# Low-rank products of a recurrent token mixer: from inside the scan to the input projection, through DRAM

## The chip, the cores and the metric

The kernel runs on one core of a Trainium2 chip. TensorE multiplies matrices into PSUM, VectorE and ScalarE work on tiles in SBUF and PSUM, GpSimd (POOL) does a few elementwise steps, and the queue of SyncE (SP) issues nearly every transfer between DRAM and SBUF. Each engine takes its instructions in a fixed order and waits on semaphores. The metric is the device time of one execution in microseconds (us), as the median of several runs.

## The reference

One layer, 2048 tokens of width 1024, in float32. The input is normed and multiplied with one input matrix; its columns are r, k, v (768 each), the low-rank inputs of decay and rate (64 each) and of the gate (128), and the queries of a small cross-attention (256). The first 2560 columns are mixed with the token before. What the change concerns:

```
log_w = -softplus(-(w0 + tanh(wd) @ w2)) - 0.5
decay = exp(-exp(log_w))
a = sigmoid(a0 + ad @ a2)
g = sigmoid(gd) @ g2
k = k * (1.0 + (a - 1.0) * k_a)
y = delta_rule_scan(r, decay, k, v, -kk, kk * a)
return (group_norm(y) * lnx_g + lnx_b + bonus) * g
```

The scan is a state of 64 x 64 in each of 12 heads, updated token by token. Scan and cross-attention go through an output matrix onto the residual stream, then an MLP of width 4096 follows.

## The kernel before

The tokens are cut three ways: 4 groups of 512 for the dense products, 16 pairs of 128 for the scan's preparation, and 32 chunks of 64 for the state update. `project(g)` multiplies a group with 22 column blocks (pz, L102, three float32r products of split operands, 24 matmuls of 512 columns a block), and `shift_store` mixes in the token before and stores a block to DRAM: r and k to rk_d, v to v_d, block 18 (decay and rate, split in a high and a low part) to lin_d, block 19 (gate) to sg_d, blocks 20 and 21 to q_d. A scheduler places every instruction by a priority number; `dense` gives the projections 1 to 3 and the output products fixed places among the pairs (`CUTS`, in steps of 640 numbers a pair), and `prepare` runs at a raised priority.

`prepare(p)` loads r (R) and k (KT) of a pair. At every second pair it loads lin for 256 tokens, multiplies it with the decay and rate matrices (pl, L324) and takes a tanh (th, L326); cs and tha are the halves of th that belong to the pair. From cs come the cumulated decay (L330 to L337), from both the operands AR and BK (L349 to L374), then the products pp (L390), a 32-step triangular inverse on VectorE (zt and Zw, L431 and L435) by way of DRAM (nd, Ti, zdr, Z), and more small products. `scan` does the two state updates (prhs, pw, pS at L485 to L498; S at L501 and L502). `post` forms the pair's result, transposes it (pty), adds a bias on ScalarE (mixT, L559), multiplies the stored gate input SG with the gate matrix in plain float32 (pg, L563) and multiplies the two on VectorE (L565). `output` multiplies by the output matrix (pout, L629). PSUM pools: psx (3 buffers) for the dense products, psa (2) for `prepare`, psy (1) for `post`. The small SBUF tiles of the projection share 7 buffers (`small`).

Of the kernel before, what the change touches and what calls it, by code (L numbers as in the profile page):

```python
# [60 lines left out]
def hybrid_layer(  # L61
# [75 lines left out]

    rk_d = [dram.tile([2 * NB, P, G], F32, name=f"rk_d{g}") for g in range(NG)]
    v_d = [dram.tile([G, MW], F32, name=f"v_d{g}") for g in range(NG)]
    lin_d = [dram.tile([2, P, G], F32, name=f"lin_d{g}") for g in range(NG)]  # L140
    sg_d = [dram.tile([P, G], F32, name=f"sg_d{g}") for g in range(NG)]
    q_d = [dram.tile([2, P, G], F32, name=f"q_d{g}") for g in range(NG)]
    mem_d = [dram.tile([P, 2, G], F32, name=f"mem_d{g}") for g in range(NG)]
    mix_d = [dram.tile([P, NB, G], F32, name=f"mix_d{g}") for g in range(NG)]
# [52 lines left out]
    bc = lambda a: a.unsqueeze(2).to_broadcast([a.shape[0], a.shape[1], HD])  # L197
    K = {}

    def scan_setup():  # L200
        K["kkc"] = col(rw_k_k[0], "kkc")
        kac = col(rw_k_a[0], "kac")
        K["lbc"] = col(rw_lnx_b[0], "lbc")
        K["ka2"] = ka2 = cb.tile([P, NB], F32, name="ka2")
        nc.vector.tensor_scalar_mul(ka2, kac, 0.5)
        K["ka1"] = ka1 = cb.tile([P, NB], F32, name="ka1")
        nc.vector.tensor_scalar(ka1, kac, -0.5, 1.0, ALU.mult, ALU.add)
        K["lgr"] = lgr = cb.tile([P, MW], F32, name="lgr")
        nc.sync.dma_start(lgr, rw_lnx_g.to_broadcast([P, MW]))

        K["lora"], K["lob"] = [], []
        for which, (w2, w0) in enumerate(((rw_w2, rw_w0), (rw_a2, rw_a0))):
            src = pr.tile([P, MW], F32, tag="kk", name="lsrc")
            for o in range(2):
                nc.sync.dma_start(src[o * HD : (o + 1) * HD], w2[0])
            wt = cb.tile([P, MW], F32R, name=f"lora{which}")
            lo = pr.tile([P, MW], F32R, tag="EM", name="llo")
            nc.scalar.copy(wt[:HD], src[:HD])
            nc.scalar.copy(lo[HD:], src[HD:])
            nc.vector.tensor_tensor(wt[HD:], src[HD:], lo[HD:].bitcast(F32), op=ALU.subtract)  # L220
            K["lora"].append(wt)
            b0 = col(w0[0], f"lob{which}")
            nc.vector.tensor_scalar_mul(b0, b0, 0.5)
            K["lob"].append(b0)

        K["sel2"] = sel2 = cb.tile([96 + NH, MW], BF16, name="sel2")
        nc.gpsimd.memset(sel2, 0.0)
# [6 lines left out]
                                    fill=0.0, base=HD - 1, channel_multiplier=HD)  # L234
        K["rn3"] = rn3 = cb.tile([96 + NH, P], BF16, name="rn3")
        nc.gpsimd.memset(rn3, 0.0)
        K["g2s"] = g2s = cb.tile([P, MW], F32, name="g2s")
        nc.sync.dma_start(g2s, rw_g2[0])
        K["rkm"] = rkm = cb.tile([P, NB, 2], F32, name="rkm")
        nc.vector.memset(rkm, 0.0)  # L240
        rk_src = rw_r_k[0].rearrange("(b two) d -> two d b", two=2)
# [39 lines left out]
    def prepare(p):  # L281
# [4 lines left out]
        nc.sync.dma_start(R, rk_d[g][:NB, :, tsl].rearrange("b p t -> p b t"))  # L286
        KT = ld.tile([P, NB, P], F32, name="KT")
        nc.sync.dma_start(KT, rk_d[g][NB:, :, tsl].rearrange("b p t -> p b t"))
        if p % 2 == 0:

            L = ld.tile([P, 2, 2, 2 * P], F32R, name="lin")
            for o in range(2):
                for part in range(2):
                    nc.sync.dma_start(L[o * HD : (o + 1) * HD, :, part, :].bitcast(F32),
                                      lin_d[g][part, :, t0 : t0 + 2 * P].rearrange("(a p) t -> p a t", p=HD))

        pss = psa.tile([96 + NH, P], F32, tag="a", name="pss")[96:]
        for b in range(NB):
# [14 lines left out]
        nc.scalar.copy(rn3[1], rn2)  # L313


        if p % 2 == 0:
            K["th"] = []
            for which in range(2):
                t = pr.tile([P, 2, NB, P], F32, name=f"th{which}")
                for b in range(NB):  # L320
                    if b % 2 == 0:
                        pz = psa.tile([P, 2, 2 * P], F32, tag="a", name="pl")
                    for part in range(2):
                        nc.tensor.matmul(pz[:, b % 2, :], K["lora"][which][:, b * P : (b + 1) * P],  # L324
                                         L[:, which, part, :], start=(part == 0), stop=(part == 1))
                    nc.scalar.activation(t[:, :, b, :], pz[:, b % 2, :].rearrange("p (j t) -> p j t", j=2),  # L326
                                         AF.Tanh, scale=0.5, bias=K["lob"][which][:, b : b + 1])
                K["th"].append(t)
        cs, tha = (t[:, p % 2] for t in K["th"])
        nc.vector.tensor_scalar_add(cs, cs, 1.0)  # L330
        for b in range(0, NB, 2):
            csh = flat(cs[:, b : b + 2, :])
# [172 lines left out]

    def post(p, d, states):
        g, t0 = p // 4, (p % 4) * P
        SG = ld.tile([P, P], F32, name="SG")
        nc.sync.dma_start(SG, sg_d[g][:, t0 : t0 + P])
        Vn = ld.tile([P, MW], F32, name="Vn")  # L510
        nc.sync.dma_start(Vn, v_d[g][t0 : t0 + P, :])
        yc = mx.tile([P, NH, HD], F32, name="yc")
# [38 lines left out]
        for q in range(2):  # L551
            bsl = slice(3 * q, 3 * q + 3)
            pt = psy.tile([P, 3, P], F32, tag="y", name="pty")
            for i in range(3):
                b = 3 * q + i
                nc.tensor.transpose(pt[:, i, :], yf[:, b * P : (b + 1) * P], ident)
            for i in range(3):
                b = 3 * q + i
                nc.scalar.activation(mixT[:, b, :], pt[:, i, :], AF.Identity, bias=K["lbc"][:, b : b + 1])  # L559
            pg = psy.tile([P, 3, P], F32, tag="y", name="pg")  # L560
            for i in range(3):
                b = 3 * q + i
                nc.tensor.matmul(pg[:, i, :], K["g2s"][:, b * P : (b + 1) * P], SG,  # L563
                                 start=True, stop=True)
            nc.vector.tensor_tensor(mixT[:, bsl, :], mixT[:, bsl, :], pg, op=ALU.mult)  # L565
        nc.sync.dma_start(mix_d[g][:, :, t0 : t0 + P], mixT)


# [65 lines left out]
    def project(g):  # L634
# [11 lines left out]
                tc.cur_priority -= UPX  # L646
            tc.cur_priority += UPX
        tail = None
        for b in range(NPB):
            w, wh, wl = weights()  # L650
            if g == 0 or (g == 1 and b >= NST):
                load_w(w, rw_in[0][:, b * P : (b + 1) * P], w_d[b] if g == 1 or b < NST else None, g == 0)
            else:
                for i in range(WQ):
                    nc.sync.dma_start(w[i].bitcast(F32), w_d[b][:, i])
            pz = psx.tile([P, G], F32, tag="x", name="pz")
            steps = mm3_steps(pz, wh, wl, lambda k: xh[k // 4][:, k % 4], lambda k: xl[k // 4][:, k % 4], KB)
            for k, _ in enumerate(steps):
                if k == 4 and tail is not None:
                    tail()  # L660
                    tail = None
                yield
            tail = shift_store(g, b, pz)
        if tail is not None:
            tail()

    def shift_store(g, b, pz):

# [15 lines left out]
        elif b < 18:  # L684
# [6 lines left out]
                c0 = (b - 12) * P  # L691
                nc.sync.dma_start(v_d[g][:, c0 : c0 + P].rearrange("(t p) c -> p t c", p=P), vt)
            return rows
        elif b == 18:
            nc.scalar.activation(sl[:HD, :], sl[:HD, :], AF.Tanh)
            hi, lo = small([P, G], "lih", F32R), small([P, G], "lil", F32R)
            split(sl, hi, lo)
            nc.sync.dma_start(lin_d[g][0], hi.bitcast(F32))
            nc.sync.dma_start(lin_d[g][1], lo.bitcast(F32))
        else:  # L700
            nc.scalar.activation(sl, sl, AF.Tanh, scale=0.5)
            nc.vector.tensor_scalar(sl, sl, 0.5, 0.5, ALU.mult, ALU.add)
            nc.sync.dma_start(sg_d[g], sl)
        return None


# [434 lines left out]
```

## Time and profile before

| | |
|---|---|
| median of 3 runs | 2777.49 us (2774.64 to 2781.78) |
| the profiled execution's own time | 2781.47 us |
| its span, first to last instruction | 2779.8 us |
| mean granted TensorE clock | 0.956 |
| TensorE busy | 2620.1 us, 94% |
| VectorE busy | 1807.5 us, 65% |
| ScalarE busy | 1410.8 us, 51% |
| DMA engines busy with the main queue | 60.0% |

Busy shares are means over stages that differ. The rows further down are read by stretches of time: an engine's busy time in a stretch, the clock granted to TensorE there (1.00 is 2.4 GHz), and what an engine waited for.

### The profile page before, as it was taken

The page shows a single profiled execution, that of the slowest core. Times are in us where ns is not written, and L with a number is a line of the kernel's source. Part 1 is how long each engine was busy: PE and PEld are TensorE (multiplying, and loading weights), DVE is VectorE, ACT ScalarE, POOL GpSimd, SP SyncE. Part 2 cuts the span into 40 slices and gives each one's busy share as a digit, 9 for nine tenths or more (in the row PEclk, how much of TensorE's full clock was granted, in tenths as well). Part 3 has the DMA queues.
Part 4 walks back from the last instruction along what each step waited for, and adds up shares of the span by engine and source line. Part 5 has one row for each costly group of instructions (what it writes and reads, how often), then busy time and mean ns, then how long its engine had stood idle before and what let it go on. Part 6 is the DMA issues. An engine that isn't in the chain of part 4 may idle for free.

```text
span 2779.8 us, 49460 instructions
## 1 busy us (share of the span) xinstructions
PE 2620.1 (94%) x17620; PEld 2131.9 (77%) x17620; DVE 1807.5 (65%) x4500; ACT 1410.8 (51%) x3053; POOL 413.1 (15%) x236
## 2 busy tenths in 40 slices
PE   6989999999899998997996999999999999999999
PEld 4777777777677777777885888878888888888887
DVE  4556657676866666778568777765875666655564
ACT  5564456465645547363446444444744444544443
POOL 2002133425304241333111000000100000000000
PEclk9999999999989988798997999999999999999999
DMA  8987564665454544335574576786775444456675
GB/s 251 286 263 215 166 176 135 168 174 165 135 152 138 144 126 120 100 86 164 160 241 133 201 260 244 275 306 191 246 258 170 145 144 155 150 192 208 211 252 167
DMA packets 468444, 519.35 MB, mean 187 GB/s; under 512 B 117538, under 2 KB 291682, under 8 KB 468196
## 3 DMA queue, kind: packets, MB, share of 16 engines
q1 hardware_dynamic: 468196, 516.18, 60.0%
q8 instruction: 139, 2.28, 0.3%
q14 instruction: 109, 0.89, 0.1%
HBM read 361.86 MB, written 154.14 MB: 186 GB/s over the span
## 4 chain that ended last, share of the span: by engine, by line
PE 74%; DMA 10%; DVE 9%; ACT 2%; issue 2%; SPq 2%; POOL 1%; DVEq 0%; ACTq 0%; POOLq 0%
PE pu L964 23%; PE py L1073 22%; PE pz L102 12%; PE pout L629 5%; PE pp L390 2%; DVE zt L431 1%; DVE Zw L435 1%; DMA zdr<-Zw 1%; PE prhs L485 1%; DMA qt<-q_d 1%; DMA KT<-rk_d 1%; DMA Z<-zdr 1%; DMA xt<-in_x_dram 1%; DMA ws<-in_rw_in_dram 1%; PE py L522 1%
## 5 line engine op out<-in xcount | busy, mean ns | idle before, releaser
L102 PE MATMUL pz<-xh,w 128*128 128x512 f32 x1408 | 484.9, 413 | 4.5 <-DVE last L681 2.7
L1073 PE MATMUL py<-wpl,hhh 128*128 128x512 f32 x896 | 349.3, 390 | 0.0
L1073 PE MATMUL py<-wph,hhl 128*128 128x512 f32 x896 | 348.3, 389 | 0.0
L1073 PE MATMUL py<-wph,hhh 128*128 128x512 f32 x896 | 344.0, 391 | 0.0
L102 PEld LDWEIGHTS pz<-xh,w 128*128 128x128 f32 x1408 | 268.9, 193 | 71.8 <-issue 6.6
L93 DVE TENSOR_TENSOR hhl<-hr,hhh 128x512 fp32r<-128x512 f32 x224 | 154.7, 691 | 225.6 <-ACT hhh L92 225.5
L92 ACT CAST hhh<-hr 128x512 fp32r<-128x512 f32 x224 | 139.1, 621 | 311.1 <-PE py L1073 295.5
L102 PE MATMUL pz<-xl,w 128*128 128x512 f32 x704 | 287.7, 409 | 0.4 <-DVE xl L93 0.4
L629 PE MATMUL pout<-wo,xh 128*128 128x256 f32 x1024 | 218.7, 307 | 18.9 <-DVE wo L93 9.6
L431 DVE TENSOR_TENSOR zt<-Ti,Zw 96x96 f32<-96x96 f32 (+20 forms) x736 | 171.2, 256 | 69.3 <-DMA Ti<-nd 49.7
L397 POOL TENSOR_TENSOR PT<-PT,msk 64x768 f32<-64x768 f32 x64 | 178.6, 2790 | 131.4 <-ACT PT L392 129.1
L629 PEld LDWEIGHTS pout<-wo,xh 128*128 128x128 f32 x1024 | 174.5, 205 | 28.9 <-DVE wo L93 12.3
L1073 PEld LDWEIGHTS py<-wph,hhl 128*128 128x128 f32 x896 | 168.4, 188 | 35.0
L1073 PEld LDWEIGHTS py<-wph,hhh 128*128 128x128 f32 x896 | 168.4, 188 | 34.8 <-DVE u L999 0.2
L1073 PEld LDWEIGHTS py<-wpl,hhh 128*128 128x128 f32 x896 | 168.4, 188 | 34.6
L435 DVE TENSOR_TENSOR Zw<-Zw,zt 96x96 f32<-96x96 f32 (+20 forms) x736 | 161.2, 242 | 6.7
L102 PEld LDWEIGHTS pz<-xl,w 128*128 128x128 f32 x704 | 135.8, 193 | 29.8 <-issue 1.9
L93 DVE TENSOR_TENSOR wpl<-wr,wph 128x512 fp32r<-128x512 f32 x224 | 153.3, 684 | 3.8 <-ACT wph L92 3.8
L629 PE MATMUL pout<-wo,xl 128*128 128x256 f32 x512 | 153.1, 299 | 0.0
L86 POOL TENSOR_TENSOR nr<-nm,nhalf 128x1 f32<-128x1 f32 x34 | 28.1, 827 | 789.2 <-DVE nm L84 736.3
L92 ACT CAST wph<-wr 128x512 fp32r<-128x512 f32 x224 | 138.2, 617 | 8.5 <-PE pu L964 7.5
L390 PE MATMUL pp<-AR,BK 64*128 64x128 f32 x768 | 94.5, 322 | 18.5 <-ACT PT L392 16.3
(293 smaller groups left out, 5640.5 us busy)
## 6 DMA issues: line engine op xcount, KB each, us to landing
w<-w_d SPq DMA_DIRECT2D x264, 256.0 KB, 4.0
hr<-hc_d SPq DMA_DIRECT2D x224, 256.0 KB, 2.8
ws<-in_w_ff_dram SPq DMA_DIRECT2D x32, 1024.0 KB, 5.7
hc_d<-hs SPq DMA_DIRECT2D x128, 256.0 KB, 2.2
wr<-t_d SPq DMA_DIRECT2D x128, 256.0 KB, 3.1
wr<-in_w_ff_dram SPq DMA_DIRECT2D x96, 256.0 KB, 3.0
w_d<-w SPq DMA_DIRECT2D x88, 256.0 KB, 4.2
ws<-in_w_out_dram SPq DMA_DIRECT2D x80, 256.0 KB, 4.3
```

The lines of the kernel that those rows point to most:

```text
L86: nc.gpsimd.tensor_tensor(t1, t0, nhalf[: ssum.shape[0], :n], op=ALU.pow)
L92: nc.scalar.copy(hi, src)
L93: nc.vector.tensor_tensor(lo, src, hi.bitcast(F32), op=ALU.subtract)
L102: nc.tensor.matmul(ps, a(k), b(k), start=(k == 0 and i == 0), stop=(k == nk - 1 and i == 2))
L390: nc.tensor.matmul(pps[q][:, j, :], BK[c][rs, b, :], d["AR"][rs, b, :], start=True, stop=True)
L397: nc.gpsimd.tensor_tensor(PT[o : o + C, :, w:], PT[o : o + C, :, w:], K["msk"][o : o + C, w:].unsqueeze(1).to_broadcast([C, NH, 2 * C - w] ...
L431: nc.vector.tensor_tensor(zt[:, j0:j1, :nt], Ti[:, s, s + 1 :].unsqueeze(1).to_broadcast([96, j1 - j0, nt]), Zw[:, j0:j1, s : s + 1].to_br ...
L435: nc.vector.tensor_tensor(Zw[:, j0:j1, s + 1 :], Zw[:, j0:j1, s + 1 :], zt[:, j0:j1, :nt], op=ALU.add)
L485: nc.tensor.matmul(pc[rs, h // 2, :], PT[:, head(h), :C], WV[:, h * HD : (h + 1) * HD], start=True, stop=True)
L629: nc.tensor.matmul(po[:, t, :], a(k, t), w[k][:, b], start=(k == 0 and i == 0 and t == 0), stop=(k == KB - 1 and i == 2 and t == 1))
L964: nc.tensor.matmul(ps, a[u][:, k * P : (k + 1) * P], b[v][:, k, :], start=(first and k == 0 and i == 0), stop=(k == 3 and i == 2), skip_gr ...
L1073: nc.tensor.matmul(ps[bk], a[u][:, m * P : (m + 1) * P], b[v], start=(fresh and c == 0 and t == 0), stop=(c == NCH - 1 and t == 2), skip_g ...
```

## The change

The products of decay, rate and gate with their low-rank matrices leave `prepare` and `post`. A new generator `low_rank(g)` does them once for a group's 512 tokens inside `project(g)`: it reads the stored block back (lw, two buffers), multiplies in psx buffers, and stores tanh and gate to DRAM (th_d, g_d). `prepare` then loads cs and tha, and `post` loads GT. The gate product is now three float32r products of split operands; so block 19 is stored in two parts too. In projections 1 to 3 blocks 18 and 19 come first, and one step of two blocks of low-rank products follows in each later block; in projection 0 the order of blocks stays, so most steps come after block 21. The part of the setup that loads the low-rank matrices moves to block 12 of projection 0.

```
-        if p % 2 == 0:
-            L = ld.tile([P, 2, 2, 2 * P], F32R, name="lin")
-            for o in range(2):
-                for part in range(2):
-                    nc.sync.dma_start(L[o * HD : (o + 1) * HD, :, part, :].bitcast(F32),
-                                      lin_d[g][part, :, t0 : t0 + 2 * P].rearrange("(a p) t -> p a t", p=HD))
+        cs = ld.tile([P, NB, P], F32, name="cs")
+        nc.sync.dma_start(cs, th_d[g][0, :, :, tsl].rearrange("b p t -> p b t"))
+        tha = ld.tile([P, NB, P], F32, name="tha")
+        nc.sync.dma_start(tha, th_d[g][1, :, :, tsl].rearrange("b p t -> p b t"))
...
-        if p % 2 == 0:
-            K["th"] = []
-            for which in range(2):
-                t = pr.tile([P, 2, NB, P], F32, name=f"th{which}")
-                for b in range(NB):
-                    if b % 2 == 0:
-                        pz = psa.tile([P, 2, 2 * P], F32, tag="a", name="pl")
-                    for part in range(2):
-                        nc.tensor.matmul(pz[:, b % 2, :], K["lora"][which][:, b * P : (b + 1) * P],
-                                         L[:, which, part, :], start=(part == 0), stop=(part == 1))
-                    nc.scalar.activation(t[:, :, b, :], pz[:, b % 2, :].rearrange("p (j t) -> p j t", j=2),
-                                         AF.Tanh, scale=0.5, bias=K["lob"][which][:, b : b + 1])
-                K["th"].append(t)
-        cs, tha = (t[:, p % 2] for t in K["th"])
...
-        SG = ld.tile([P, P], F32, name="SG")
-        nc.sync.dma_start(SG, sg_d[g][:, t0 : t0 + P])
+        GT = ld.tile([P, NB, P], F32, name="GT")
+        nc.sync.dma_start(GT, g_d[g][:, :, t0 : t0 + P].rearrange("b p t -> p b t"))
...
-            pg = psy.tile([P, 3, P], F32, tag="y", name="pg")
-            for i in range(3):
-                b = 3 * q + i
-                nc.tensor.matmul(pg[:, i, :], K["g2s"][:, b * P : (b + 1) * P], SG,
-                                 start=True, stop=True)
-            nc.vector.tensor_tensor(mixT[:, bsl, :], mixT[:, bsl, :], pg, op=ALU.mult)
+            nc.vector.tensor_tensor(mixT[:, bsl, :], mixT[:, bsl, :], GT[:, bsl, :], op=ALU.mult)
...
-        for b in range(NPB):
+        low = None
+        for b in list(range(NPB)) if g == 0 else [18, 19] + list(range(18)) + [20, 21]:
+            if g == 0 and b == 12:
+                low_rank_setup()
...
+                if k == 6 and low is not None:
+                    next(low, None)
                 yield
             tail = shift_store(g, b, pz)
+            if b == 19:
+                low = low_rank(g)
+        for _ in low:
+            pass
...
+    def low_rank(g):
+        def pair(hi, lo, rows):
+            t = [ep.tile([P, G], F32R, tag="lw", name="lw", bufs=2) for _ in range(2)]
+            for u, src in zip(t, (hi, lo)):
+                for o in range(0, P, rows):
+                    nc.sync.dma_start(u[o : o + rows].bitcast(F32), src)
+            return t
+        for which in range(2):
+            rs = slice(which * HD, which * HD + HD)
+            xin = pair(lin_d[g][0, rs], lin_d[g][1, rs], HD)
+            for b in range(NB):
+                pl = psx.tile([P, G], F32, tag="x", name="pl")
+                for part in range(2):
+                    nc.tensor.matmul(pl, K["lora"][which][:, b * P : (b + 1) * P], xin[part],
+                                     start=(part == 0), stop=(part == 1))
+                t = small([P, G], "th")
+                nc.scalar.activation(t, pl, AF.Tanh, scale=0.5, bias=K["lob"][which][:, b : b + 1])
+                nc.sync.dma_start(th_d[g][which, b], t)
+                if b % 2 == 1:
+                    yield
+        gin = pair(lin_d[g][2], lin_d[g][3], P)
+        for b in range(NB):
+            pg = psx.tile([P, G], F32, tag="x", name="pg")
+            bs = slice(b * P, (b + 1) * P)
+            for i, (u, v) in enumerate(((0, 0), (0, 1), (1, 0))):
+                nc.tensor.matmul(pg, K["g2"][u][:, bs], gin[v], start=(i == 0), stop=(i == 2))
+            t = small([P, G], "gt")
+            nc.scalar.copy(t, pg)
+            nc.sync.dma_start(g_d[g][b], t)
+            if b % 2 == 1:
+                yield
```

The scheduler decides where these instructions come to stand. On SP's queue at the start of the scan, the program before has this order (lin is the low-rank input of pairs 0 and 1, w the weights and xt the rows of x for projection 1):

```order
L703 DMA sg_d_79<-sl 128x512
L294 DMA lin<-lin_d_75 64x2x256 x2
...
L655 DMA w<-w_d_151 128x512 x4
L655 DMA w<-w_d_152 128x512 x2
L640 DMA xt<-in_x_dram 128x1024
L655 DMA w<-w_d_152 128x512 x2
L672 DMA q_d_83<-sl 128x512
L640 DMA xt<-in_x_dram 128x1024
```

The changed program has this order there; lw is the stored low-rank input, th_d the stored tanh, g_d the stored gate, cs, tha and GT their loads for the pairs:

```order
L665 DMA lw<-lin_d_75 64x512 x4
L295 DMA cs<-th_d_79 128x6x128
L678 DMA th_d_79<-th 128x512 x3
L665 DMA lw<-lin_d_75 128x512 x2
L678 DMA th_d_79<-th 128x512 x3
L297 DMA tha<-th_d_79 128x6x128
L689 DMA g_d_83<-gt 128x512 x6
L623 DMA xt<-in_x_dram 128x1024
L295 DMA cs<-th_d_79 128x6x128
L497 DMA GT<-g_d_83 128x6x128
L293 DMA KT<-rk_d_67 128x6x128
L623 DMA xt<-in_x_dram 128x1024
```

The last two loads of x for projection 1 have moved behind group 0's low-rank loads and stores, and the very last one behind the second pair's cs and the first pair's GT.

On TensorE at the same place, from the last low-rank product to the first pair's pp, the program before has:

```order
L324 MATMUL pl<-lin,lora_1952 128x256 x10
L160 MATMUL pt<-ident,xt 128x128 x8
...
L160 MATMUL pt<-ident,xt 128x128 x4
L102 MATMUL pz<-xh,w 128x512
...
L102 MATMUL pz<-xh,w 128x512
L390 MATMUL pp<-AR,BK 128x128 x6
```

and the changed one:

```order
L674 MATMUL pl<-lw,lora_1172 128x512 x12
L510 MATMUL py_7096<-S,AR 64x64
L686 MATMUL pg<-lw,g2h 128x512 x4
...
L161 MATMUL pt<-ident,xt 128x128 x16
L378 MATMUL pp<-AR,BK 128x128 x6
L393 MATMUL psb<-rkm,tha 64x2 x12
...
L161 MATMUL pt<-ident,xt 128x128 x4
L102 MATMUL pz<-xh,w 128x512
```

Before, 31 matmuls of the next projection (pz) stand ahead of the first pp; now none does, and the gate products stand there. Further on, the scan has moved forward against the dense work: of 384 pS matmuls 264 stood ahead of the last pz and now 288 do, and of the output's matmuls (pout) 692 stood behind the last pS and now 1095 do.

## Rows read from the trace of the kernel before

**Rows 1.** The page, part 1: busy us (share of the span) x instructions.
```profile
PE 2620.1 (94%) x17620; PEld 2131.9 (77%) x17620; DVE 1807.5 (65%) x4500; ACT 1410.8 (51%) x3053; POOL 413.1 (15%) x236
```
**Rows 2.** Busy time by stretches: length, PE, PEld, DVE, ACT, POOL (x instructions), PEclk, DMA share, GB/s.
```profile
190.30:1051.00 860.70, 811.52 (x7498) 629.82 (x7495) 570.64 (x2012) 460.27 (x1142) 269.45 (x137) 0.95 0.56 159
1051.00:1383.50 332.50, 295.88 (x3125) 257.44 (x3126) 234.17 (x722) 171.30 (x446) 98.96 (x44) 0.84 0.44 123
1383.50:1469.00 85.50, 78.87 (x686) 76.68 (x683) 51.58 (x118) 36.11 (x94) 10.32 (x7) 1.00 0.80 250
```
**Rows 3.** The same of tile S alone: PE, PEld, DVE, ACT.
```profile
1051.00:1383.50 332.50, 11.21 (x216) 8.69 (x216) 10.47 (x20) 9.21 (x18) 0.84 0.44 123
```
**Rows 4.** The same of tile pout alone: PE, PEld, DVE.
```profile
1051.00:1383.50 332.50, 141.51 (x844) 123.55 (x844) 11.62 (x17) 0.84 0.44 123
```
**Rows 5.** The chain of work that ended last: start us, us, what.
```profile
159.99 5.62 PE pz L102 x24
...
1432.33 15.28 PE pout L629 x125
```
**Rows 6.** Groups by line and form: busy us, mean ns | idle before, releasers.
```profile
L324 PE MATMUL pl<-lin,lora 128*128 128x256 f32 x192 | 44.8, 331 | 7.9 <-ACT th L326 6.0 <-DMA lin<-lin_d 1.7
...
L326 ACT ACTIVATE th<-pl,lob 128x256 f32<-128x256 f32 x96 | 43.1, 478 | 17.7 <-PE pl L324 17.4
...
L563 PE MATMUL pg<-SG,g2s 128*128 128x128 f32 x192 | 31.0, 299 | 0.7 <-ACT mixT L559 0.7
...
L565 DVE TENSOR_TENSOR mixT<-mixT,pg 128x384 f32<-128x384 f32 x32 | 17.5, 548 | 38.7 <-PE pg L563 31.0 <-ACT Z L467 6.7 <-issue 0.5
```
**Rows 7.** Timeline of PE, 578 to 594 us: start us, us, engine, line.
```profile
592.88 0.71 PE L324 MATMUL pl<-lin,lora 128*128 128x256 f32 x4
593.53 0.70 PE L772 MATMUL psco<-kTm,qt 64*128 64x256 f32 x4
```
**Rows 8.** Timeline of PE, 363 to 372 us.
```profile
365.27 0.95 PE L563 MATMUL pg<-SG,g2s 128*128 128x128 f32 x6
365.98 0.48 PE L102 MATMUL pz<-xl,w 128*128 128x512 f32 x1
366.30 0.62 PE L102 MATMUL pz<-xh,w 128*128 128x512 f32 x2
```
**Rows 9.** Busy time by stretches of tile lin, then of tile SG: PE, PEld.
```profile
1051.00:1383.50 332.50, 6.73 (x30) 4.40 (x29) 0.84 0.44 123
...
1051.00:1383.50 332.50, 9.71 (x60) 8.06 (x60) 0.84 0.44 123
```
**Rows 10.** Groups by line and form of ACT.
```profile
L701 ACT ACTIVATE sl<-sl 128x512 f32<-128x512 f32 x4 | 2.5, 630 | 1.2 <-DVE last L681 1.0 <-DVE sl L676 0.2
```
**Rows 11.** DMA issues: xcount, KB each, median us to landing.
```profile
rk_d<-sl SPq DMA_DIRECT2D x48, 256.0 KB, 3.8
...
KT<-rk_d SPq DMA_DIRECT2D x16, 384.0 KB, 4.8
...
lin<-lin_d SPq DMA_DIRECT2D x32, 128.0 KB, 3.0
```
**Rows 12.** Timeline of DVE at four places.
```profile
312.25 1.02 DVE L330 TENSOR_SCALAR th<-th 128x768 f32<-128x768 f32 x2
...
446.77 0.55 DVE L502 TENSOR_TENSOR S<-S,ec 128x384 f32<-128x384 f32 x1
...
1325.60 0.55 DVE L502 TENSOR_TENSOR S<-S,ec 128x384 f32<-128x384 f32 x1
...
1365.81 0.55 DVE L502 TENSOR_TENSOR S<-S,ec 128x384 f32<-128x384 f32 x1
```
**Rows 13.** Timeline of SP's queue, 176 to 206 us.
```profile
193.74 0.33 SPq L640 DMA_DIRECT2D xt<-in_x_dram  x1
```
**Rows 14.** Timeline of PE, 203 to 219 us.
```profile
209.84 0.78 PE L102 MATMUL pz<-xh,w 128*128 128x512 f32 x1
```

More of the change, by code (lines that the diff above doesn't have):

```diff
@@ L139, in hybrid_layer @@
     v_d = [dram.tile([G, MW], F32, name=f"v_d{g}") for g in range(NG)]
-    lin_d = [dram.tile([2, P, G], F32, name=f"lin_d{g}") for g in range(NG)]
-    sg_d = [dram.tile([P, G], F32, name=f"sg_d{g}") for g in range(NG)]
+    lin_d = [dram.tile([4, P, G], F32, name=f"lin_d{g}") for g in range(NG)]
+    th_d = [dram.tile([2, NB, P, G], F32, name=f"th_d{g}") for g in range(NG)]
+    g_d = [dram.tile([NB, P, G], F32, name=f"g_d{g}") for g in range(NG)]
     q_d = [dram.tile([2, P, G], F32, name=f"q_d{g}") for g in range(NG)]
@@ L198, in hybrid_layer, with low_rank_setup @@
     K = {}
[L200 to L209, printed above, removed]
+    def low_rank_setup():
         K["lora"], K["lob"] = [], []
@@ L224, in scan_setup @@
             K["lob"].append(b0)
+        src = pr.tile([P, MW], F32, tag="kk", name="lsrc")
+        nc.sync.dma_start(src, rw_g2[0])
+        K["g2"] = [cb.tile([P, MW], F32R, name=f"g2{p}") for p in "hl"]
+        split(src, *K["g2"])
+    def scan_setup():
+        K["kkc"] = col(rw_k_k[0], "kkc")
+        kac = col(rw_k_a[0], "kac")
+        K["lbc"] = col(rw_lnx_b[0], "lbc")
+        K["ka2"] = ka2 = cb.tile([P, NB], F32, name="ka2")
+        nc.vector.tensor_scalar_mul(ka2, kac, 0.5)
+        K["ka1"] = ka1 = cb.tile([P, NB], F32, name="ka1")
+        nc.vector.tensor_scalar(ka1, kac, -0.5, 1.0, ALU.mult, ALU.add)
+        K["lgr"] = lgr = cb.tile([P, MW], F32, name="lgr")
+        nc.sync.dma_start(lgr, rw_lnx_g.to_broadcast([P, MW]))
         K["sel2"] = sel2 = cb.tile([96 + NH, MW], BF16, name="sel2")
@@ L236, in scan_setup @@
         nc.gpsimd.memset(rn3, 0.0)
-        K["g2s"] = g2s = cb.tile([P, MW], F32, name="g2s")
-        nc.sync.dma_start(g2s, rw_g2[0])
         K["rkm"] = rkm = cb.tile([P, NB, 2], F32, name="rkm")
@@ L693, in shift_store @@
             return rows
-        elif b == 18:
-            nc.scalar.activation(sl[:HD, :], sl[:HD, :], AF.Tanh)
+        else:
+            if b == 18:
+                nc.scalar.activation(sl[:HD, :], sl[:HD, :], AF.Tanh)
+            else:
+                nc.scalar.activation(sl, sl, AF.Tanh, scale=0.5)
+                nc.vector.tensor_scalar(sl, sl, 0.5, 0.5, ALU.mult, ALU.add)
             hi, lo = small([P, G], "lih", F32R), small([P, G], "lil", F32R)
             split(sl, hi, lo)
[L698 to L703, printed above, removed]
+            for i, t in enumerate((hi, lo)):
+                nc.sync.dma_start(lin_d[g][2 * (b - 18) + i], t.bitcast(F32))
         return None
```

## The prediction

> **What bounds the kernel now.** I read the page first: TensorE is busy 94% of the span, VectorE 65% [rows 1]. Then busy time by stretches, cut where the program changes character [rows 2]: the projection of group 0 (0 to 190.3 us), the projections of groups 1 to 3 woven into the scan (to 1051), the last part of the scan with output products between (to 1383.5), the output products left over (to 1469), and the MLP. The reader should see two kinds of stretch. From 190.3 to 1051 TensorE is busy 811.5 of 860.7 us at a granted clock of 0.95: there its queue is the bound, and what leaves it is gained. From 1051 to 1383.5 it is busy 295.9 of 332.5 us, but at 0.84, so the scan's own waits set part of the pace. In the leftover output products it is busy 78.9 of 85.5 us at 1.00. The change touches nothing behind 1469, so I leave that part as it is.
>
> A chunk is one state update, two VectorE instructions on S. The stretch from 1051 to 1383.5 holds 20 of them (10 chunks) [rows 3]: 332.5 / 10 = 33.25 us a chunk. It also holds 844 output matmuls in 141.5 us, 0.168 us each; a run of 125 at full clock takes 15.28 us, 0.122 us each [rows 4, 5].
>
> **Change 1: matmuls.** Removed from the scan: 192 matmuls of 256 columns (pl) and 192 instructions, two to a call, of the f32 gate product (pg) [rows 6]. By starts in the timeline, four pl hold the queue 0.65 us (592.88 to 593.53) [rows 7] and six pg 0.71 us (365.27 to 365.98) [rows 8]: 48 x 0.65 + 32 x 0.71 = 53.9 us. Added: 4 groups x (24 + 18) = 168 matmuls of 512 columns. The trace has the same shape in pz, 24 in 5.62 us [rows 5], 0.234 each: 39.4 us, and 0.09 us more where the queue changes operands (365.98 to 366.30 took 0.32 for one pz) in 72 places, 6.5 us: 45.9 us. In sum TensorE loses 8 us of work; at the low clock both sides would cost up to twice that, which bounds it at 16. By place: 30 pl and 60 pg stood between 1051 and 1383.5 [rows 9], 7.5 x 0.65 + 10 x 0.71 = 12 us, and the last two groups of pg behind that, 1.4 us; so the stretch to 1051 loses 40.5 us and takes up all 45.9: +5.4 us there.
>
> **Change 2: ScalarE and VectorE.** 96 tanh of 0.478 us go [rows 6]; 48 of 512 columns and 24 copies come, at 0.63 us like the tanh of that shape [rows 10]: 45.9 us out, 45.4 in. Nothing is charged for ScalarE, nor for the four more splits (some 0.6 us each on it and on VectorE, under TensorE's work). The gate's multiply on VectorE stays, but it no longer waits for pg, for which VectorE stood still 31.0 us [rows 6]. VectorE is not the bound, and the same multiply still waits for ScalarE's mixT; I credit 0, and the bound is 31 us if each of these waits held up the chain.
>
> **Change 3: DRAM traffic.** Per pair three loads of 384 KB (cs, tha, GT) in place of SG and, at every second pair, four lin loads; per group 18 stores of 256 KB: some 38 MB more, on a stretch whose DMA engines are 0.56 and 0.44 busy [rows 2]. A load of this shape (KT) lands in 4.8 us [rows 11]. A pair's first decay work stands far ahead of its state update (L330 of pairs 2 and 3 at 312, the first S of pair 2 at 447 [rows 12]), which covers 5 us of landing; at no cover it would be 16 x 4.8 = 77 us. SP issues 116 more transfers, at 0.33 us like the x load [rows 13] some 38 us of issue, spread over 1280 us. Of the bounds, 0 and 77 us, I take the lower, since the row of pair 2 leaves 135 us for 5; 12 us stay in the range for weights held up behind a cs load that waits for its buffer.
>
> **Change 4: the start of the scan.** Here the change adds a wait on the path. For group 0 the products come after the last projection block, so the scan's first pair must wait for store, load, product, store, load. On SP the x rows of projection 1 (the last two xt loads) stand behind all of that in the order shown above, the last one behind a cs load that waits for pair 0's use of its buffer. Before, the last was issued at 193.74, and pz of group 1 began at 209.84 [rows 13, 14]. Now: the last block is done near 194; lw of the rate can be loaded only when the decay's products have read its two buffers, four issues and 3.0 us landing, 200; six tanh of 0.63 us, 204; store 3.8 and tha load 4.8 us with their issues, 213.5; VectorE's three products of pair 0 that free cs, some 4 us with their hops, 218. The last x load follows, lands in 4 to 5 us, and norm, transpose and split take some 6 (193.74 to 209.84 held all of it before, 16 us): pz near 230, 20 us later than before. Of these 20 us TensorE fills about 10 (gate products 18 x 0.234 = 4.2, the rest pair 0's work pulled forward). So +10 us, between 2 (if the loads slip in) and 20 (if nothing fills). The Trainium skill, "DMA: Bandwidth & Descriptors", section "Anatomy of one DMA", speaks against such a round trip: a transfer has a fixed cost near 2 us, most of it the receipt of a write, dearest for HBM. By its formula four transfers in a row would take an estimated 4 x 2.5 = 10 us; the rows give 3.8 + 3.0 + 3.8 + 4.8 = 15.4 [rows 11], and the sum goes by the rows.
>
> **Change 5: the order of scan and output.** A pair now has fewer instructions, while the output's places are fixed numbers, so the scan runs ahead. Counted in the two orders: 264 of 384 pS calls stood ahead of the last pz, now 288, which is two chunks; and of the output's matmuls 692 stood behind the last pS, now 1095, so 403 move to the end. A chunk's own TensorE time is (295.9 - 141.5 - 12) / 10 = 14.2 us. The stretch to the last pz thus takes 860.7 + 28.5 (two chunks) + 5.4 + 10 = 904.6 us. Then 8 chunks and 441 output matmuls. If idle time per chunk stays, (332.5 - 295.9) / 10 = 3.7 us, they take 8 x (14.2 + 3.7) + 441 x 0.168 = 217 us, 27 a chunk. If the scan is paced by its own chain, 8 x 33.25 = 266 us. The trace shows the last pair 40 us behind the one before it (1325.60 to 1365.81) [rows 12], while the mean is 66.5, so either is possible; I take the middle, 241. The end takes 85.5 - 1.4 + 403 x 0.122 = 133 us.
>
> **The sum**: 190.3 + 904.6 + 241 + 133 = 1468.9 against 1469: no change. The profiled execution took 2781.5 (span 2779.8), 4.0 above the median of the three runs, 2777.5; the forecast stands against that median: 2777.
>
> **Rivals.** *Faster: the chain has slack.* Speaking for it: the last pair at 40 us, and VectorE freed of the pg waits. Against: the clock of 0.84. The late stretch then takes 217: -24, or 2753. *Slower: the scan loses its cover.* In its last 8 chunks 55 output matmuls stand between two updates, where there were 84. If 33.25 us a chunk is the chain's own latency, TensorE idles instead: 266 us, +25, or 2802. It decides when a chunk takes more than 30 us. Idle time there also comes with the low clock: 0.84 in this stretch, against 1.00 where the output products run alone [rows 2]. "TensorE: Matmul & The Clock Gate" of the Trainium skill, "What's actually happening", says the same: throttled by default, released by activity. *No move at all: start and gain cancel and the pace is as before*, which is my forecast's middle, so it is not counted apart. *The start costs 20 us and SP's queue holds weights up by the 12*: +22, or 2799; against it, the sum of the issues is small.
>
> **Chances.** Forecast (within some 15 us of 2777): 0.42, of which 0.12 faster, 0.2 within the 0.3% (8 us) that a measurement tells from no change, 0.1 slower. Slack: 0.27. Lost cover: 0.21. Start and queue: 0.10. So faster 0.39, same 0.20, slower 0.41. The range goes from the slack case with a part of VectorE's waits and the clock's share of change 1, 2745, to the lost cover with a dearer start, 2811.
>
> **What would show it.** Change 1: pl and pg at 0.23 to 0.26 us each, and none behind the last pz. Change 4: pz of group 1 first near 230, pp of pair 0 near 220. Change 5: the last S update earlier than 1383 (near 1336), some 1095 pout behind it, and between the last pz and it a pace between 27 and 33 us a chunk; the granted clock there tells which rival it was. The prediction is wrong if TensorE's idle time grows in the stretch to 1051 (weights or PSUM buffers late), since I charge nothing for that.

## The result, and the profile after

The changed kernel takes 2876.49 us (median of 4 runs, 2864.66 to 2881.93) against 2776.84 before: a ratio of 1.0351, 95% interval 1.0314 to 1.0387. It is 100 us slower, where no change was forecast, and lies outside the range.

Page of the changed kernel, part 1 (busy us, share of the span, instructions):

```profile
PE 2655.8 (92%) x17404; PEld 2150.3 (75%) x17404; DVE 1849.7 (64%) x4505; ACT 1416.1 (49%) x3034; POOL 408.1 (14%) x236
```

Busy time by stretches of the changed kernel, cut at the places that answer to [rows 2]: the last pz, the last update of S, and the point that stands as far ahead of the MLP as 1469 did before. Columns: length, PE, PEld, DVE, ACT, POOL (x instructions), PEclk, DMA share, GB/s.

```profile
190.30:1212.20 1021.90, 918.27 (x7890) 706.40 (x7890) 668.77 (x2173) 509.01 (x1240) 301.18 (x150) 0.88 0.60 175
1212.20:1428.00 215.80, 182.68 (x2171) 158.00 (x2170) 156.63 (x514) 110.82 (x288) 61.75 (x31) 0.81 0.49 131
1428.00:1575.00 147.00, 127.13 (x1055) 125.55 (x1054) 73.22 (x171) 54.76 (x136) 10.16 (x7) 0.93 0.71 221
```

The whole loss stands in the first row. Up to the last pz the program needs 1021.9 us, 161 more than the 860.7 before [rows 2]; behind it 362.8 us to the mark, 55 fewer than 418. With 5.6 us less behind the mark this is the 100.4 us between the spans of the two profiled executions.

In that stretch three things grew. TensorE was idle 103.6 us (1021.9 - 918.27) and 49.2 before. Its granted clock fell from 0.95 to 0.88: as the levels are 1.2 and 2.4 GHz, that is some 245 us at 1.2 GHz (2 x 0.12 x 1021.9) against 86. With each matmul weighed by the clock of its moment, 115 us of TensorE's busy time were lost to the low clock where 37 had been, 78 more. The work itself, weighed so, grew from 775 to 803 us, 28 more. The forecast had counted work, and 10 us for the start.

The start is the smaller part. Busy time from 190.3 us to the first pz of group 1, in the changed kernel and in the kernel before:

```profile
190.30:246.36 56.06, 36.04 (x162) 27.82 (x162) 26.89 (x38) 29.16 (x65) 9.26 (x5) 0.68 0.68 227
```

```profile
190.30:209.84 19.54, 10.38 (x53) 8.26 (x51) 12.39 (x23) 13.58 (x30) 1.21 (x2) 0.70 0.66 218
```

TensorE was idle 20.0 us there, and 9.2 before. Of the 54 us by which its idle time grew, 44 stand behind the start.

Idle time and low clock belong together. Timeline of TensorE in the changed kernel around one short wait (start us, us, instruction; in brackets the idle time ahead of it and what ended it):

```profile
656.48 0.54 PE L686 MATMUL pg<-lw,g2h 128*128 128x512 f32 x1 [4.01 <-DVE last L707]
656.94 1.65 PE L378 MATMUL pp<-AR,BK 64*128 64x128 f32 x6
...
673.00 1.26 PE L378 MATMUL pp<-AR,BK 64*128 64x128 f32 x12
```

The busy time around it:

```profile
640.00:652.00 12.00, 9.97 (x91) 8.24 (x90) 8.96 (x33) 5.01 (x12) 2.72 (x2) 1.00 0.65 174
652.00:670.00 18.00, 13.98 (x64) 10.70 (x64) 7.15 (x16) 9.17 (x22) 8.47 (x5) 0.63 0.86 269
```

TensorE stood still 4.0 us, and over the 18 us with that stop and behind it the clock is 0.63: six pp take 1.65 us there, while twelve take 1.26 at 673. So this wait is paid twice. Counted in the timeline from 190 us to the last pz, TensorE stood still for more than 1 us 36 times (87 us in all), and 14 times (38 us) before. Only six of the 36 (23 us) stand right ahead of pl and pg; the other 30 stand ahead of instructions that the kernel before has too.

What pg waited for shows why such waits are hard to foresee. Timelines of ScalarE and then VectorE at the same place:

```profile
652.38 0.69 ACT L302 ACTIVATE sq<-KT,kkc 128x128 f32<-128x128 f32 x2 [6.28 <-DMA KT<-rk_d]
...
654.73 0.67 ACT L701 ACTIVATE sl<-pz,omc 128x512 f32<-128x512 f32 x1
```

```profile
655.43 0.75 DVE L702 SCALAR_TENSOR_TENSOR sl<-pz,muc,sl 128x511 f32<-128x511 f32 x1 [6.30 <-ACT sl L701]
...
656.22 0.15 DVE L707 COPY last<-pz 128x1 f32<-128x1 f32 x1
```

pg needs a psx buffer. The buffer still holds a finished pz, which VectorE reads last; VectorE waits for ScalarE, and ScalarE stands in front of a KT load of the next pair. ScalarE and VectorE, each in its own order, hand the wait for one load on to TensorE.

### The profile page after: what moved, and what is told of

Its sections match the earlier page's. It is cut to its first block, busy times and chain, and to the rows that moved or that the text cites. A ratio compares the mean times of both kernels' runs of the same rounds, so it can differ in the third digit from the quotient of the medians.

```text
span 2880.2 us, 49325 instructions
## 1 busy us (share of the span) xinstructions
PE 2655.8 (92%) x17404; PEld 2150.3 (75%) x17404; DVE 1849.7 (64%) x4505; ACT 1416.1 (49%) x3034; POOL 408.1 (14%) x236
## 4 chain that ended last, share of the span: by engine, by line
PE 63%; DVE 10%; DMA 10%; ACT 4%; issue 4%; SPq 2%; POOL 0%; DVEq 0%; ACTq 0%; POOLq 0%
PE pu L990 22%; PE py L1099 21%; PE pz L102 6%; PE pout L612 5%; DVE zt L419 2%; DVE Zw L423 2%; DMA tha<-th_d 1%; PE pp L378 1%; DMA ws<-in_w_out_dram 1%; DMA KT<-rk_d 1%; DMA zdr<-Zw 1%; PE prhs L473 1%; DMA cs<-th_d 1%; PE pe L454 1%; PE psco L798 1%
## 5 line engine op out<-in xcount | busy, mean ns | idle before, releaser
L102 PE MATMUL pz<-xh,w 128*128 128x512 f32 x1408 | 501.8, 424 | 6.7 <-ACT xh L92 2.2
L102 PEld LDWEIGHTS pz<-xh,w 128*128 128x128 f32 x1408 | 279.5, 200 | 81.3 <-issue 7.0
L102 PE MATMUL pz<-xl,w 128*128 128x512 f32 x704 | 294.3, 418 | 0.2 <-DVE xl L93 0.2
L612 PE MATMUL pout<-wo,xh 128*128 128x256 f32 x1024 | 207.7, 300 | 32.7 <-ACT wo L92 27.6
L423 DVE TENSOR_TENSOR Zw<-Zw,zt 96x96 f32<-96x96 f32 (+20 forms) x736 | 169.0, 251 | 7.0
```

What stands on the lines that cost most here:

```text
L102: nc.tensor.matmul(ps, a(k), b(k), start=(k == 0 and i == 0), stop=(k == nk - 1 and i == 2))
L423: nc.vector.tensor_tensor(Zw[:, j0:j1, s + 1 :], Zw[:, j0:j1, s + 1 :], zt[:, j0:j1, :nt], op=ALU.add)
L612: nc.tensor.matmul(po[:, t, :], a(k, t), w[k][:, b], start=(k == 0 and i == 0 and t == 0), stop=(k == KB - 1 and i == 2 and t == 1))
```

## The experiments

Each version was timed beside the kernel before, and the ratio is to its runs there. Differences to the changed kernel are to its 2876.5 us, beside which the kernel before took 2776.8; beside the versions it took 2778 to 2783, so such a difference is good to some 5 us. Each edit also makes the scheduler sort the instructions anew, so that a few us of any difference may be due to the new order.

**First round: buffers, start, traffic.** The first theory was that cs and tha, with one buffer each, make every pair wait. VectorE's waits for them in the changed kernel (us in total, times, longest):

```profile
DVE cs L318 <- DMA cs<-th_d: 46.1, 11, 27.0
...
DVE cs L337 <- DMA tha<-th_d: 28.7, 11, 7.0
```

`lora_only`: post has the gate product of before again, low_rank keeps decay and rate.

```
-        GT = ld.tile([P, NB, P], F32, name="GT")
...
+        SG = ld.tile([P, P], F32, name="SG")
...
+                nc.tensor.matmul(pg[:, i, :], K["g2s"][:, b * P : (b + 1) * P], SG,
```

> Only the decay and rate products move (cs and tha come from DRAM into one buffer each); the gate product stays with its pair as before. Buffer theory (a pair's cs and tha loads wait until the pair before has used up the one buffer, and VectorE then waits for the landing): most of the 100 us stay, 2835 to 2865 us, with VectorE still waiting 40 us or more for cs and tha. Order theory (the fixed places of the output products thin the cover of the scan; 849 of 1536 pout stand behind the last state update here, 1095 in the changed kernel, 692 before): about two fifths of the loss, 2815 us. Start theory: the 30 us of the start stay, and little else, 2800 to 2810 us.

Measured: 2799.8 us, ratio 1.0062 (1.0039 to 1.0085). Only 17 of 100 us are left, though VectorE waits as long as in the changed kernel: 51.3 us for cs and 31.2 for tha.

`lora_dbl`: the same with

```
+        cs = ld.tile([P, NB, P], F32, name="cs", bufs=2)
...
+        tha = ld.tile([P, NB, P], F32, name="tha", bufs=2)
```

> The same with two buffers for cs and for tha; nothing else differs, but the order of instructions follows (817 pout behind the last state update). Buffer theory: the waits for cs and tha go from VectorE (under 15 us) and 40 us or more go from the time: 2785 to 2810 us, what is left being the start. Order theory: as with one buffer, within 10 us of it. Start theory: as with one buffer.

Measured: 2797.2 us, 1.0059 (1.0040 to 1.0077). The wait for tha went from 31.2 to 1.6 us, the one for cs stayed at 50.9, and the time did not move. The buffer theory falls: VectorE has room for tha's waits, and those for cs do not come from the one buffer. What they cost is not shown.

`after_start`:

```
-        for b in list(range(NPB)) if g == 0 else [18, 19] + list(range(18)) + [20, 21]:
-            if g == 0 and b == 12:
+        for b in [18, 19] + list(range(18)) + [20, 21]:
+            if g == 0 and b == 18:
```

> The changed kernel, with blocks 18 and 19 first in projection 0 too, so that group 0's low-rank products are done within projection 0 and not behind it. Start theory: the first pz of group 1 comes back from 242 us to near 215, and 30 to 50 us of the 100 go: 2825 to 2845 us. Buffer theory: the start gives at most 20 us, 2855 to 2876 us, as the later pairs are paced by their own loads.

Measured: 2873.9 us, 1.0326 (1.0288 to 1.0364), no gain. The first pz of group 1 came at 256.6 us, later than the 246.4 of the changed kernel: projection 0 was held up instead, and its last pz began at 234.0 us in place of 197.5.

`b_traffic`:

```
+        for u in range(3):
+            cp = dram.tile([P, NB, P], F32, tag="cp", name="cp", bufs=3)
+            nc.sync.dma_start(cp, rk_d[g][NB:, :, tsl].rearrange("b p t -> p b t"))
```

> The kernel before, with three copies of 384 KB from DRAM to DRAM added in each pair on SP's queue, which nothing reads: about the change's extra traffic (38 MB with reads and writes) and 48 more transfers to issue. Traffic theory: 2815 us or more. Buffer, order and start theories: within 15 us of the kernel before, 2765 to 2795 us.

Measured: 2823.4 us, 1.0141 (1.0098 to 1.0184). Copies that nothing waits for cost 41 us, as the traffic theory said, so transfers on SP's queue are not free. Whether the bytes or the issues cost was not separated.

**Second round: the order, and the gate's parts.** As the gate's move made up most of the loss, it was taken apart.

`after_p520`:

```
-LAG = 3
-PAIR_RANKS = 640
+LAG = 0
+PAIR_RANKS = 520
```

> The changed kernel with the dense work's places pulled forward (PAIR_RANKS 520 and LAG 0 in place of 640 and 3), which puts 264 pS ahead of the last pz, as in the kernel before, and 326 pout behind the last pS; the arithmetic and the transfers are the same. Order theory (projections fall behind a scan that runs ahead of them in the queue, TensorE idles in the scan's gaps and its clock falls): the last pz comes 60 us or more earlier than 1212 us and the time falls to 2790 to 2830 us. Theory of the gate's traffic and products as such: within 20 us of the changed kernel, 2855 to 2890 us.

Measured: 2891.7 us, 1.0405 (1.0378 to 1.0431). With 264 pS ahead of the last pz, as before, the time does not come back. The stretch to the last pz:

```profile
190.30:1176.50 986.20, 884.68 (x7542) 670.90 (x7542) 608.23 (x2065) 485.54 (x1176) 279.31 (x140) 0.90 0.63 177
```

That is 36 us less than in the changed kernel, but 125.5 more than before, and TensorE was idle 101.5 us of it. The last pairs then ran late. Behind the last pz the order is not that of before (326 pout behind the last pS, and 692 before). So it is not the scan's running ahead that costs ahead of the last pz; as far as this order tests it, the order theory falls.

`gt_noprod`: the gate part of low_rank is left out, and

```
-        nc.sync.dma_start(GT, g_d[g][:, :, t0 : t0 + P].rearrange("b p t -> p b t"))
+        nc.sync.dma_start(GT, rk_d[g][NB:, :, t0 : t0 + P].rearrange("b p t -> p b t"))
```

> The changed kernel without the gate's products, their copies and their stores; GT is loaded as before, but from the stored k in place of the gate (so the output has the wrong gate). Theory that the added products, copies and stores in the projection's stretch cost: the time falls to 2800 to 2820 us, near the kernel that moves decay and rate alone (2800). Theory that the GT loads of 384 KB a pair cost: it stays above 2850 us.

Measured: 2790.4 us, 1.0033 (1.0016 to 1.0050). Its stretch to the last pz:

```profile
190.30:1125.50 935.20, 859.33 (x7706) 658.39 (x7705) 599.43 (x2108) 483.06 (x1184) 279.07 (x141) 0.90 0.63 179
```

Without the gate's products, copies and stores 86 us go, more than either theory said: 28 of idle time (75.9 against 103.6), 20 of work, and the rest by the clock. This version is 8 us slower than the kernel before, though by the page it still moves 31 MB more through DRAM, of the 40 MB more that the changed kernel moves. So it is not the traffic alone that costs.

`gt_once`:

```
...
+        if p == 0:
+            K["GT"] = ld.tile([P, NB, P], F32, name="GT")
...
+        GT = K["GT"]
```

> The changed kernel with GT loaded for the first pair alone and used for all (so the gate is the wrong one for 15 of 16 pairs); products, copies and stores stay. Theory that the products and stores cost: above 2850 us. Theory that the loads cost: 2800 to 2825 us.

Measured: 2879.9 us, 1.0358 (1.0338 to 1.0378). The 15 loads cost nothing here.

**Third round: products or stores.** `gt_nostore` loads GT as gt_noprod does and has one line less than the changed kernel:

```
-            nc.sync.dma_start(g_d[g][b], t)
```

> The changed kernel with the gate's products and copies, but without the 24 stores of the gate; GT is loaded from the stored k instead (so the gate is the wrong one). Product theory (the 72 matmuls, with their loads of lw and their PSUM buffers, cost where the projections are the bound): 2850 to 2880 us. Store theory (the stores hold up SP's queue or the small buffers): 2790 to 2815 us.

Measured: 2840.4 us, 1.0209 (1.0184 to 1.0234), between the two expectations.

`gt_storeonly`, also with GT from k, has no lw loads and no matmuls for the gate, and

```
-            nc.scalar.copy(t, pg)
+            nc.scalar.copy(t, K["lora"][0][:, :G].bitcast(F32))
```

> The changed kernel without the gate's 72 matmuls and their loads of lw, but with 24 copies by ScalarE (from a weight tile) and the 24 stores (so the gate is the wrong one). Product theory: 2785 to 2810 us, as without copies and stores (2790). Store theory: 2840 us or more. If both parts cost about half, 2820 to 2840 us.

Measured: 2818.4 us, 1.0127 (1.0100 to 1.0155). So products with copies cost 50 us over gt_noprod, and copies with stores 28. The copies are in both, so the two do not split the 86 us. Neither theory is right alone. Of their own the 72 matmuls take 17 us and the 24 copies 13.9.

`after_fine`, in both loops of low_rank:

```
-                if b % 2 == 1:
-                    yield
+                yield
```

> The changed kernel with one block of low-rank products a step in place of two (18 steps a group in place of 9), so that a step holds one of the three psx buffers and not two. Theory that the pairs of products crowd out pz from its PSUM buffers and bunch the work: 2820 to 2855 us. Theory that only the amount of work added to the stretch counts: within 12 us of the changed kernel, 2865 to 2890 us.

Measured: 2869.6 us, 1.0317 (1.0285 to 1.0348). The size of a step does not matter beyond 7 us.

**Fourth round: what in the gate's work costs.** `gt_1of3`:

```
-            for i, (u, v) in enumerate(((0, 0), (0, 1), (1, 0))):
-                nc.tensor.matmul(pg, K["g2"][u][:, bs], gin[v], start=(i == 0), stop=(i == 2))
+            nc.tensor.matmul(pg, K["g2"][0][:, bs], gin[0], start=True, stop=True)
```

> The changed kernel with one of the three matmuls of each gate product (so the gate lacks its small parts): 48 of 72 matmuls of 512 columns go, 11 us of TensorE at full clock; loads, copies, stores and places stay. Theory that TensorE's time counts once: 8 to 15 us below the changed kernel, 2860 to 2868 us. Theory that added TensorE time costs about three times itself: 2835 to 2850 us. Theory that the round trip and not the matmuls costs: within 6 us of it, 2870 to 2882 us.

Measured: 2843.4 us, 1.0221 (1.0180 to 1.0263): 33 us for 11 us of matmuls. Up to the last pz its profile has 12 us less idle time and 32 us less lost to the low clock than the changed kernel's, and no less work.

`after_dve`:

```
-            nc.scalar.copy(t, pg)
+            nc.vector.tensor_copy(t, pg)
```

> The changed kernel with the gate's 24 copies on VectorE in place of ScalarE. Theory that ScalarE's order (a copy holds up the scan's evictions) costs: 2850 us or less. Otherwise within 15 us of the changed kernel, 2861 to 2891 us.

Measured: 2853.6 us, 1.0256 (1.0221 to 1.0291). 23 us go, between the two expectations.

`gate_late`: low_rank(0) ends behind decay and rate, its gate part becomes gate(g), and

```
-        low = None
+        low = gate(0) if g == 1 else None
...
-                low = low_rank(g)
+                low = chain(low or (), low_rank(g))
```

> The changed kernel with group 0's gate products taken from the end of projection 0 into the first blocks of projection 1. Start theory: the first pz of group 1 comes at 230 us in place of 246, and 15 us or more go, 2845 to 2862 us. Theory that only the amount of work added ahead of the last pz counts: within 12 us of the changed kernel.

Measured: 2840.8 us, 1.0210 (1.0167 to 1.0253). The first pz of group 1 came at 230.0 us, 16 earlier, and 36 us went.

`after_actq`:

```
-                nc.sync.dma_start(th_d[g][which, b], t)
+                nc.scalar.dma_start(th_d[g][which, b], t)
...
-            nc.sync.dma_start(g_d[g][b], t)
+            nc.scalar.dma_start(g_d[g][b], t)
```

> The changed kernel with the 72 stores of tanh and gate issued from ScalarE's own queue, behind the activation that makes them, in place of SP's. Queue theory (on SP each store waits for ScalarE, 53 us in all, and behind it wait the scan's round trips through DRAM and the weights): SP's waits for ScalarE's th and gt go, and the time falls by 30 us or more, to 2810 to 2846 us. Other theories: within 12 us of the changed kernel, or slower, as ScalarE issues now.

Measured: 2865.4 us, 1.0294 (1.0251 to 1.0337). SP's waits ahead of these stores, in the changed kernel

```profile
SPq L678 <- ACT th L677: 34.5, 25, 5.6
...
SPq L689 <- ACT gt L688: 18.7, 12, 3.9
```

are gone, and 11 us at most with them. The queue is a small part.

**Fifth round: is it the stretch or the waits?** `b_extra`, on the kernel before:

```
+            if g > 0 and b < 18:
+                for i in range(3):
+                    nc.tensor.matmul(pz, wh(0), xh[0][:, i], start=True, stop=True)
```

> The kernel before with 162 more matmuls of 512 columns in projections 1 to 3 (three ahead of each of the blocks 0 to 17, into the same PSUM buffer, overwritten by the block's own): 38 us of TensorE at full clock, no transfer, no copy, no wait, same output. Theory that TensorE time in this stretch costs about three times itself, as the projections' end holds up the scan: 2860 to 2900 us. Theory that it counts once: 2810 to 2830 us. Theory that the scan's own chain bounds the stretch: under 2800 us.

Measured: 2812.0 us, 1.0118 (1.0085 to 1.0151): 32 us for 38. Its stretch to the last pz:

```profile
190.30:1093.90 903.60, 865.74 (x7974) 671.66 (x7975) 564.62 (x2031) 469.60 (x1164) 280.54 (x142) 0.95 0.55 153
```

TensorE was idle 37.9 us there, less than the 49.2 before, at the same clock of 0.95. Matmuls that wait for no load and need no eviction of their own count once. So TensorE's time as such is not what costs three times itself in the gate's products; it is idle time and clock, as in gt_1of3. Why fewer matmuls bring fewer waits there was not found.

`late_dve`: the edits of gate_late and after_dve together.

> The changed kernel with both: group 0's gate products in projection 1, and the copies on VectorE. If the two add up (36 and 23 us): 2810 to 2825 us. If both give back the same wait: 2830 to 2845 us.

Measured: 2836.8 us, 1.0201 (1.0146 to 1.0256). They do not add up.

`lora_lw4`: lora_only with

```
+            t = [ep.tile([P, G], F32R, tag="lw", name="lw", bufs=4) for _ in range(2)]
```

> Decay and rate moved alone, with four lw buffers in place of two, so that at the start the rate's loads needn't wait for the decay's products. Start theory: the first pz of group 1 comes at 220 us or earlier in place of 229, and the time falls from 2800 to 2785 to 2792 us. Otherwise 2795 to 2805 us.

Measured: 2807.6 us, 1.0094 (1.0067 to 1.0122). At the start TensorE's wait of 6.4 us for lw went, but one of 7.6 us for AR took its place; the first pz came at 224.9 in place of 229.3, and nothing was gained.

`after_ahead`:

```
             xin = pair(lin_d[g][0, rs], lin_d[g][1, rs], HD)
+            yield
...
         gin = pair(lin_d[g][2], lin_d[g][3], P)
+        yield
```

> The changed kernel with the loads of lw issued one step, that is one block of the projection, ahead of the first products that read them (12 steps a group in place of 9, the same instructions). Theory of the short waits: TensorE's waits for lw behind 260 us (13 us before the edit) go, the half-clock time behind them goes as well, and the time falls by 25 us or more, to 2830 to 2850 us. Otherwise, if such waits only turn up elsewhere, within 15 us of the changed kernel.

Measured: 2852.5 us, 1.0267 (1.0238 to 1.0296): 24 us less. Of the changed kernel's waits for lw, such as

```profile
313.10 1.19 PE L674 MATMUL pl<-lw,lora 128*128 128x512 f32 x2 [5.03 <-DMA lw<-lin_d]
```

with a clock of 0.60 between 308 and 329 us, none is left behind 260 us. Yet TensorE's idle time to the last pz, which ends at 1185.0, is as before the edit (103.5 us), and so is its work; other waits took their place, and the gain is in the clock, 0.89: 86 us lost to it in place of 115. The result falls between the two expectations.

No version here beats the kernel before.

## Why the prediction was wrong

**The step that failed** is the sum of Change 5, "The stretch to the last pz thus takes 860.7 + 28.5 (two chunks) + 5.4 + 10 = 904.6 us". It measured 1021.9. Apart from the 10 us of the start, the forecast took TensorE's idle time and clock over from before and added work. The work came nearly as forecast (28 us more where 28.5 + 5.4 were added). Idle time grew by 54 us, 44 of them behind the start, and the time at 1.2 GHz by some 160, which cost 78. The prediction named this as what would make it wrong, "since I charge nothing for that", but gave it no rival and no chance, and no price but 12 us for late weights; its range ended at 2811, the lost cover with a dearer start.

**What bounds the kernel.** "What leaves it is gained" holds, the other way round, for pure TensorE time (b_extra, 32 us for 38). It doesn't hold for a product with a load ahead of it, a PSUM buffer and an eviction behind it: 17 us of matmuls with their copies and stores made 86 us (gt_noprod).

**Change 1.** The sizes were right: four pl at full clock hold the queue 0.92 us (286.38 to 287.30), 0.23 each.

**Change 2.** ScalarE at nothing was too low: with the gate's copies on VectorE 23 us went (after_dve). Its busy time is nearly the same, but the order isn't: it stood still 42.2 us for pl ahead of th and 12.6 for pg ahead of gt, where it had waited 17.4 for pl [rows 6]. The credit of 0 for VectorE was right: the gate's multiply now waits 39.4 us for ScalarE's mixT in place of 38.7 in all [rows 6].

**Change 3.** The loads of tha and GT are covered, as forecast (lora_dbl, gt_once); for cs, whose waits stayed in lora_dbl, this is not shown, but decay and rate with all that they bring cost 17 us (lora_only). What the stores and issues cost wasn't covered: 28 us for copies and stores (gt_storeonly), and 36 us went without the gate's stores (gt_nostore).

**Change 4.** The mechanism was right and the size wrong: pz of group 1 began at 246.4 us, 36.5 later than before, where 230 was forecast. Half of the 16 us were lost ahead of the last x load, which went out at 226.2 us and not at 218 (tha was in at 220.0, where 213.5 was forecast). The other half was lost behind it: the last transpose of x waited for VectorE's split, which stood behind AR products of the second pair. Three of these took 1.83, 2.17 and 3.83 us, where the first pair's took 0.55; GpSimd ran multiplies beside them. Timelines of SP, VectorE, GpSimd and TensorE:

```profile
226.19 0.35 SPq L623 DMA_DIRECT2D xt<-in_x_dram  x1
```

```profile
240.25 3.83 DVE L362 TENSOR_TENSOR AR<-R,E 128x384 f32<-128x384 f32 x1
```

```profile
237.86 5.79 POOL L385 TENSOR_TENSOR PT<-PT,msk 64x768 f32<-64x768 f32 x2
```

```profile
245.60 1.12 PE L161 MATMUL pt<-ident,xt 128*128 128x128 f32 x4 [4.57 <-DVE xl L93]
246.36 0.78 PE L102 MATMUL pz<-xh,w 128*128 128x512 f32 x1
```

Up to that pz TensorE lost 11 us more than before by idle time and 9 by the clock, together the upper end of the forecast's 2 to 20. Moving group 0's gate products away gave the 16 us back, and 36 in all (gate_late). The formula of the Trainium skill that the prediction quotes here stands in a section on transfers issued by GpSimd, and the ones here are SP's; nothing in the sum rests on it.

**Change 5.** Behind the last pz the sum was nearly right: 362.8 us against 241 + 133 = 374. That is luck in part, as two errors offset each other. Eight chunks took 215.8, 27.0 each, where 241 was forecast; this is the end that the rival "the chain has slack" named, and "lost cover" (266) is refuted. The end took 147.0 where 133 was forecast, at a clock of 0.93 and not 1.00. The reason given for the new order, places that are fixed numbers, agrees with after_p520: with other numbers 264 pS stand ahead of the last pz again. The time did not come back with them.

**What is shown, and what stays open.** It is shown that the loss stands ahead of the last pz as idle time and half-clock time; that the gate's products, copies and stores make 86 of the 100 us and the rest of the change some 8 to 14; and that a second buffer for tha, GT's loads, the number of pS ahead of the last pz and the size of the steps do not. More psx or `small` buffers were not tried. Four edits that touch different parts of the gate's work (fewer matmuls, copies on VectorE, a later place, earlier loads) each gave back 23 to 36 us, and two together 40. Edits that leave the work as it is (after_start, after_p520, after_fine) moved the time by -3, +15 and -7 us. That speaks for many short waits that hand on to each other, as in the row at 656 us, rather than for one; which of them would have to go for the whole 86 us was not found, nor why most of the stops stand ahead of instructions that were there before. How much of a difference of some 10 us is due to the order that each edit brings was not tried.

## What to carry to other kernels

Price a moved product with its load, its PSUM buffer and its eviction, not by its matmuls: where TensorE is busy 94% and several in-order queues hand buffers to each other, each new link can stop it. Count waits over 1 us on TensorE and read the granted clock behind them: here the stop of 4 us was followed by half clock, and all in all the clock cost more than the idle time itself (78 us and 54). Where a range rests on idle time staying as it is, give its growth a rival of its own.

## What the hardware showed beside this

The gate's multiply on VectorE reads both operands from SBUF now, one of them from PSUM before. Its mean rose from 548 ns [rows 6] to 882, and the longest from 0.56 to 3.49 us. All five long ones (1.6 us and more) start while GpSimd runs a multiply and end 0.42 us behind its end. Before, five of the multiplies met an instruction of GpSimd too and took 0.56 us at most. Timelines of VectorE and of GpSimd:

```profile
683.88 3.40 DVE L548 TENSOR_TENSOR mixT<-mixT,GT 128x384 f32<-128x384 f32 x1 [4.90 <-ACT mixT L547]
```

```profile
681.50 5.37 POOL L385 TENSOR_TENSOR PT<-PT,msk 64x768 f32<-64x768 f32 x2 [5.62 <-ACT PT L380]
```

The Trainium skill, "SBUF — State Buffer", section "SBUF: two separate sides", says that VectorE with two SBUF inputs and GpSimd share a pair of ports which the first comer holds for its whole instruction. These rows agree. The cost in this multiply is small: 32 of them took 28.2 us in place of 17.5. The AR products at the start, 0.55 us and then up to 3.83, read two SBUF operands as well.
